# RMSNorm and SiLU: 1/rms by ScalarE's Sqrt and VectorE's reciprocal instead of GpSimd's pow

## The chip, the cores and the metric

One core of a Trainium2 chip. The metric is device time in microseconds for one execution of the program. PE is TensorE, DVE is VectorE, ACT is ScalarE, POOL is GpSimd, and SP is SyncE, which here issues loads. ACTq and SPq are the instruction queues of ACT and SP where they issue DMAs.

## The reference

```python
def reference(x, gamma, eps):          # x: 8 x 1024 x 2048 float32, gamma: 2048, eps: 1e-5
    rms = np.sqrt(np.mean(x ** 2, axis=-1, keepdims=True) + eps)
    out = gamma * x / rms
    return (out * (1 / (1 + np.exp(-out)))).astype(np.float32)
```

Each of 8192 rows of 2048 numbers is divided by its root mean square and scaled by gamma, and SiLU is applied to the result.

## The kernel before

The 8192 rows are cut into 16 blocks of 512 rows. A block is one tile `xt` of 128 partitions, each with J = 4 rows of 2048 numbers side by side: 4096 KB. There are six such buffers, and everything happens in place in them. A block is loaded by one DMA that SP issues (`load`, L52) and stored by one DMA that ACT issues (`store`, L91); only the last block is stored in two halves (L88).

`sums(b)` makes the sum of squares of each row. Its rows are shared out: the first `na` rows go to ACT (Square with an accumulated sum, into the PSUM tile `junk_a`, L68), the others to DVE (a multiply with an accumulated sum, into `junk_v`, L64). `na` is 2, but 3 in blocks 1, 5, 9 and 13. The four sums are in `ss`, 128x4. POOL then computes `var = ss / 2048 + eps` (L74) and `rstd = var ** -0.5` (L77, with a constant tile `half` that holds -0.5).

`finish(b)` multiplies each row by its rstd and by gamma on DVE (`scalar_tensor_tensor`, L82, four per block); after every second row ACT applies Silu to the two rows together (L86, 128x4096, two per block).

The order is written out by hand, and each engine works through its own instructions in that order:

```python
for b in range(1, last - 1):
    sums(b + 1, after_first=[b - 1])
    finish(b)
```

So the sums of block b+1, and its rstd, come ahead of the scaling of block b: rstd is there one block ahead. The store of block b-1 is issued by ACT just after its first square of block b+1, and when a store has landed, SP can issue the load of the block six further on, into the same buffer. At the start six loads are issued (the sixth after gamma has been spread over all partitions by TensorE, with `grow` in the sixth buffer). At the end the order is: store 13, finish 14, store 14, sums 15, finish 15 with its two halves.

Of the kernel before, what the change touches and what calls it, by code (L numbers as in the profile page):

```python
# [1 line left out]

# [4 lines left out]

ACT = mybir.ActivationFunctionType
ALU = mybir.AluOpType


@with_exitstack
def kernel(
    ctx: ExitStack,
    tc: tile.TileContext,
    x: bass.AP,
    gamma: bass.AP,
    eps: bass.AP,
    out: bass.AP,
):  # L20

    nc = tc.nc
    P = nc.NUM_PARTITIONS
    f32 = mybir.dt.float32
    x2 = x.flatten_outer_dims()
    o2 = out.flatten_outer_dims()  # L30
    n, d = x2.shape
    J = 4
    BUFS, LEAD = 6, 6
    nblk = n // (P * J)
    xb = x2.rearrange("(b p j) d -> b p (j d)", p=P, j=J)
    ob = o2.rearrange("(b p j) d -> b p (j d)", p=P, j=J)

    singles = ctx.enter_context(tc.tile_pool(name="singles", bufs=1))
    pool = ctx.enter_context(tc.tile_pool(name="pool", bufs=BUFS))
    small = ctx.enter_context(tc.tile_pool(name="small", bufs=2))  # L40
    psum = ctx.enter_context(tc.tile_pool(name="psum", bufs=1, space=bass.MemoryType.PSUM))

    g = singles.tile([P, d], f32)
    half = singles.tile([P, J], f32)
    ones = singles.tile([P, P], f32)
    junk_a = psum.tile([P, d], f32, name="junk_a")
    junk_v = psum.tile([P, d], f32, name="junk_v")
    blocks, rstds = {}, {}

    def load(b):  # L50
        xt = pool.tile([P, J * d], f32, name="xt")
        nc.sync.dma_start(out=xt, in_=xb[b])  # L52
        blocks[b] = xt

    def row(b, j):
        return blocks[b][:, j * d:(j + 1) * d]

    def sums(b, after_first=()):


        ss = small.tile([P, J], f32, name="ss")
        na = J - 1 if b % 4 == 1 else J - 2
        for j in range(na, J):
            nc.vector.tensor_tensor_reduce(  # L64
                out=junk_v, in0=row(b, j), in1=row(b, j), scale=1.0, scalar=0.0,
                op0=ALU.mult, op1=ALU.add, accum_out=ss[:, j:j + 1])
        for j in range(na):
            nc.scalar.activation(out=junk_a, in_=row(b, j), func=ACT.Square,  # L68
                                 accum_out=ss[:, j:j + 1])
            if j == 0:  # L70
                for s in after_first:
                    store(s)
        var = small.tile([P, J], f32, name="var")
        nc.gpsimd.tensor_scalar(out=var, in0=ss, scalar1=1.0 / d, scalar2=float(eps),  # L74
                                op0=ALU.mult, op1=ALU.add)
        rstd = small.tile([P, J], f32, name="rstd")
        nc.gpsimd.tensor_tensor(out=rstd, in0=var, in1=half, op=ALU.pow)  # L77
        rstds[b] = rstd

    def finish(b, halves=False):  # L80
        for j in range(J):
            nc.vector.scalar_tensor_tensor(out=row(b, j), in0=row(b, j), scalar=rstds[b][:, j:j + 1],  # L82
                                           in1=g, op0=ALU.mult, op1=ALU.mult)
            if j % 2:
                cols = slice((j - 1) * d, (j + 1) * d)
                nc.scalar.activation(out=blocks[b][:, cols], in_=blocks[b][:, cols], func=ACT.Silu)  # L86
                if halves:
                    nc.scalar.dma_start(out=ob[b][:, cols], in_=blocks[b][:, cols])  # L88

    def store(b):  # L90
        nc.scalar.dma_start(out=ob[b], in_=blocks[b])  # L91
        if b + LEAD < nblk:
            load(b + LEAD)

    with tc.manual_schedule():


        Q = 4
        w = d // Q
        grow = pool.tile([P, J * d], f32, name="xt")  # L100
        for b in range(BUFS - 1):
            load(b)
        nc.vector.memset(ones, 1.0)  # L103
        nc.gpsimd.memset(half, -0.5)  # L104
        nc.scalar.activation(out=junk_a[:, 0:1], in_=ones[:, 0:1], func=ACT.Square)  # L105
        nc.scalar.dma_start(out=grow[0:P:P // Q, 0:w],
                            in_=bass.AP(tensor=gamma.tensor, offset=gamma.offset, ap=[[w, Q], [1, w]]))
        for c in range(Q):
            k = c * (P // Q)
            nc.tensor.matmul(junk_v[:, c * w:(c + 1) * w], ones[k:k + 1, :], grow[k:k + 1, 0:w],  # L110
                             start=True, stop=True)
        nc.vector.tensor_copy(out=g, in_=junk_v)  # L112
        load(BUFS - 1)


        last = nblk - 1
        sums(0)
        finish(0)
        sums(1)
        for b in range(1, last - 1):  # L120
            sums(b + 1, after_first=[b - 1])
            finish(b)
        store(last - 2)
        finish(last - 1)
        store(last - 1)
        sums(last)
        finish(last, halves=True)


# [1 line left out]
_INS = ['x', 'gamma', 'eps']  # L131
_OUTS = [((8, 1024, 2048), 'float32')]

_NUMBERS = {'eps': 9.999999747378752e-06}


# [26 lines left out]
```

## Time and profile before

| what | value |
|---|---|
| median of 9 runs | 317.86 us (317.4 to 318.82) |
| profiled execution | 318.03 us, of which 315.9 us is the span of the profile |
| DVE busy | 212.6 us, 67% |
| ACT busy | 190.3 us, 60% |
| POOL busy | 64.6 us, 20% |
| moved by DMA | 134.24 MB, mean 425 GB/s |
| table loads on ACT | 2, 1.283 us each |

The span runs from the first instruction to the last. Busy shares are means over it. A row of the groups gives the line, the engine, the operation, its tiles and shapes, how often it ran, and the mean duration of one.

### The profile page before, as it was taken

How to read it: one execution, taken by the hardware profiler on the slowest of the kernel's cores; microseconds unless marked ns; L12 is line 12 of the kernel's file. 1: busy time of each engine (PE TensorE's matmuls, PEld its weight loads, DVE VectorE, ACT ScalarE, POOL GpSimd, SP SyncE). 2: the span in 40 equal slices, each digit the busy share in tenths (PEclk: the TensorE clock that was granted, in tenths of full speed). 3: DMA queues.
4: the chain of work that ended last, by engine and by line, in shares of the span. 5: the costliest groups of instructions: out<-in, count | busy, mean ns of one | idle time of the engine just before them, and what ended most of it. 6: DMA issues, size and time to landing. Idle time of an engine off the chain costs nothing.

```text
span 315.9 us, 446 instructions
## 1 busy us (share of the span) xinstructions
PE 2.1 (1%) x8; PEld 0.5 (0%) x8; DVE 212.6 (67%) x122; ACT 190.3 (60%) x107; POOL 64.6 (20%) x37
## 2 busy tenths in 40 slices
PE   0200000000000000000000000000000000000000
PEld 0000000000000000000000000000000000000000
DVE  0688699996672956929577294893939549993700
ACT  1338978688774295463877438557378843784620
POOL 0010160514040500605104060140601306001000
DMA  8999999999999999999999999999999999999996
GB/s 333 411 452 423 440 398 415 448 436 427 448 415 452 408 445 419 448 415 448 415 461 407 456 415 448 415 452 427 436 427 436 427 436 431 432 440 423 444 409 280
DMA packets 4762, 134.24 MB, mean 425 GB/s; under 512 B 532, under 2 KB 532, under 8 KB 536
## 3 DMA queue, kind: packets, MB, share of 16 engines
q1 hardware_dynamic: 2304, 67.11, 49.6%
q10 hardware_dynamic: 2456, 67.12, 49.3%
q14 instruction: 2, 0.02, 0.0%
HBM read 67.12 MB, written 67.11 MB: 425 GB/s over the span
## 4 chain that ended last, share of the span: by engine, by line
DMA 69%; DVE 9%; ACT 3%; issue 2%; DVEq 1%; POOLq 0%; ACTq 0%; POOL 0%; SPq 0%
DMA xt<-in_x_dram 37%; DMA out_dram<-xt 32%; DVE xt L82 8%; ACT xt L86 2%; ACT junk_a L68 1%; DVE junk_v L64 1%; DVEq L158 1%; POOLq L158 0%; ACTq L91 0%; DVE ss L64 0%; POOL var L74 0%; ACTq L68 0%; SPq L52 0%; DVEq L82 0%; DVEq L64 0%
## 5 line engine op out<-in xcount | busy, mean ns | idle before, releaser
L86 ACT ACTIVATE xt<-xt 128x4096 f32<-128x4096 f32 x32 | 115.8, 3618 | 71.4 <-DVE xt L82 71.4
L82 DVE SCALAR_TENSOR_TENSOR xt<-xt,rstd,g 128x2048 f32<-128x2048 f32 x64 | 146.1, 2347 | 8.7 <-POOL rstd L77 8.7
L64 DVE CUSTOM_DVE_ANT_0 junk_v<-xt 128x2048 f32<-128x2048 f32 x28 | 64.4, 2300 | 67.1 <-DMA xt<-in_x_dram 66.6
L68 ACT ACTIVATE junk_a<-xt 128x2048 f32<-128x2048 f32 x36 | 67.7, 1880 | 39.6 <-DMA xt<-in_x_dram 38.5
L74 POOL TENSOR_SCALAR var<-ss 128x4 f32<-128x4 f32 x16 | 22.4, 1401 | 222.7 <-DVE ss L64 118.1
L77 POOL TENSOR_TENSOR rstd<-var,half 128x4 f32<-128x4 f32 x16 | 41.9, 2621 | 1.3
L112 DVE COPY g<-junk_v 128x2048 f32<-128x2048 f32 x1 | 2.3, 2293 | 9.3 <-PE junk_v L110 9.3
L68 ACT ACTIVATION_READ_ACCUMULATOR junk_a<-xt 128x1 f32 x36 | 6.7, 187 | 0.0
L64 DVE DVE_READ_ACCUMULATOR2_ANT ss<- 128x1 f32 x28 | 4.0, 142 | 0.0
L110 PE MATMUL junk_v<-xt,ones 1*128 1x512 f32 x8 | 2.1, 1132 | 8.1 <-DMA xt<-in_gamma_dram 8.1
L105 ACT ACT_TABLE_LOAD x1 | 1.3, 1283 | 0.7 <-PEq L144 0.7
L86 ACT ACT_TABLE_LOAD x1 | 1.3, 1283 | 0.0
L103 DVE MEMSET ones<- 128x128 f32 x1 | 0.2, 165 | 0.8 <-PEq L144 0.8
L110 PEld LDWEIGHTS junk_v<-xt,ones 1*128 1x128 f32 x8 | 0.5, 305 | 8.1 <-issue 8.1
L105 ACT ACTIVATE junk_a<-ones 128x1 f32<-128x1 f32 x1 | 0.2, 174 | 0.0
L104 POOL MEMSET half<- 128x4 f32 x1 | 0.1, 102 | 0.3 <-POOLq L144 0.3
L144 POOL MEMSET const-float32-0.0<- 128x1 f32 x1 | 0.1, 99 | 0.2 <-issue 0.2
L144 POOL MEMSET const-bfloat16-1.0<- 128x1 bf16 x1 | 0.1, 102 | 0.0
L144 POOL MEMSET const-uint8-127<- 128x1 uint8 x1 | 0.1, 102 | 0.0
L144 POOL MEMSET const-float32-1.0<- 128x1 f32 x1 | 0.1, 99 | 0.0
## 6 DMA issues: line engine op xcount, KB each, us to landing
xt<-in_x_dram SPq DMA_DIRECT2D x16, 4096.0 KB, 38.4
out_dram<-xt ACTq DMA_DIRECT2D x15, 4096.0 KB, 38.6
out_dram<-xt ACTq DMA_DIRECT2D x2, 2048.0 KB, 12.6
xt<-in_gamma_dram ACTq DMA_DIRECT2D x1, 8.0 KB
```

The source lines that it names most:

```text
L64: nc.vector.tensor_tensor_reduce(out=junk_v, in0=row(b, j), in1=row(b, j), scale=1.0, scalar=0.0, op0=ALU.mult, op1=ALU.add, accum_out=ss[ ...
L68: nc.scalar.activation(out=junk_a, in_=row(b, j), func=ACT.Square, accum_out=ss[:, j:j + 1])
L74: nc.gpsimd.tensor_scalar(out=var, in0=ss, scalar1=1.0 / d, scalar2=float(eps), op0=ALU.mult, op1=ALU.add)
L77: nc.gpsimd.tensor_tensor(out=rstd, in0=var, in1=half, op=ALU.pow)
L82: nc.vector.scalar_tensor_tensor(out=row(b, j), in0=row(b, j), scalar=rstds[b][:, j:j + 1], in1=g, op0=ALU.mult, op1=ALU.mult)
L86: nc.scalar.activation(out=blocks[b][:, cols], in_=blocks[b][:, cols], func=ACT.Silu)
L103: nc.vector.memset(ones, 1.0)
L105: nc.scalar.activation(out=junk_a[:, 0:1], in_=ones[:, 0:1], func=ACT.Square)
L110: nc.tensor.matmul(junk_v[:, c * w:(c + 1) * w], ones[k:k + 1, :], grow[k:k + 1, 0:w], start=True, stop=True)
L112: nc.vector.tensor_copy(out=g, in_=junk_v)
L144: nc = _bacc.Bacc("TRN2", target_bir_lowering=False, num_devices=1)
L158: with _tile.TileContext(nc) as tc:
```

## The change

POOL's two operations are replaced. ACT computes `rms = sqrt(ss / 2048 + eps)` at the end of `sums` (eps is a one-column tile, set once by DVE), and a new function `invert` has DVE take the reciprocal. In the loop `invert(b + 1)` stands after `finish(b)`; for blocks 0, 1 and 15 it stands just after `sums`. All blocks now have two rows of squares on ACT and two on DVE. POOL keeps only the constants that the program's start sets.

```diff
-    half = singles.tile([P, J], f32)
+    eps_t = singles.tile([P, 1], f32)
...
-        na = J - 1 if b % 4 == 1 else J - 2
+        na = J // 2
...
-        var = small.tile([P, J], f32, name="var")
-        nc.gpsimd.tensor_scalar(out=var, in0=ss, scalar1=1.0 / d, scalar2=float(eps),
-                                op0=ALU.mult, op1=ALU.add)
+        rms = small.tile([P, J], f32, name="rms")
+        nc.scalar.activation(out=rms, in_=ss, func=ACT.Sqrt, scale=1.0 / d, bias=eps_t)
+        rmss[b] = rms
+
+    def invert(b):
         rstd = small.tile([P, J], f32, name="rstd")
-        nc.gpsimd.tensor_tensor(out=rstd, in0=var, in1=half, op=ALU.pow)
+        nc.vector.reciprocal(out=rstd, in_=rmss.pop(b))
         rstds[b] = rstd
...
-        nc.gpsimd.memset(half, -0.5)
+        nc.vector.memset(eps_t, float(eps))
...
         sums(0)
+        invert(0)
         finish(0)
         sums(1)
+        invert(1)
         for b in range(1, last - 1):
             sums(b + 1, after_first=[b - 1])
             finish(b)
+            invert(b + 1)
         store(last - 2)
         finish(last - 1)
         store(last - 1)
         sums(last)
+        invert(last)
         finish(last, halves=True)
```

More of the change, by code (lines that the diff above doesn't have):

```diff
@@ L47 @@
     junk_v = psum.tile([P, d], f32, name="junk_v")
-    blocks, rstds = {}, {}
+    blocks, rmss, rstds = {}, {}, {}
     def load(b):
```

## The prediction

> **What bounds the kernel now.** I read the page's busy shares first, then its slices, then stretches of the span by windows, then the order of time inside one block and at the end.
>
> Busy time of each engine, from the page, and the busy share of the 16 DMA engines in 40 slices:
>
> ```profile
> PE 2.1 (1%) x8; PEld 0.5 (0%) x8; DVE 212.6 (67%) x122; ACT 190.3 (60%) x107; POOL 64.6 (20%) x37
> DMA  8999999999999999999999999999999999999996
> ```
>
> No compute engine is full; the DMA engines are, from the second slice to the last but one. 134.24 MB must pass. The windows (busy us by engine, clock, DMA share, GB/s) say how full:
>
> ```profile
> 10.00:38.00 28.00, 0.23 (x4) 0.00 (x0) 23.14 (x15) 18.41 (x13) 1.21 (x2) 1.00 1.01 437
> 38.00:62.00 24.00, 0.00 (x0) 0.00 (x0) 22.54 (x12) 18.78 (x12) 10.58 (x6) 1.00 0.99 415
> 100.80:256.80 156.00, 0.00 (x0) 0.00 (x0) 104.98 (x60) 93.94 (x52) 38.03 (x16) 1.00 1.00 433
> ```
>
> 437 GB/s while only loads run, 415 when the first stores join, 433 for the long middle. A block is one load and one store of 4096 KB, 8.39 MB, and 8.39 MB at 433 GB/s is 19.4 us. The middle runs at just that pace, as the order of time of one block shows (start, length, what; the idle time before it in brackets):
>
> ```profile
> 198.86 1.88 ACT L68 ACTIVATE junk_a<-xt 128x2048 f32<-128x2048 f32 x1 [1.91 <-DMA xt<-in_x_dram]
> 198.89 2.30 DVE L64 CUSTOM_DVE_ANT_0 junk_v<-xt 128x2048 f32<-128x2048 f32 x1 [5.58 <-DMA xt<-in_x_dram]
> 203.50 9.14 DVE L82 SCALAR_TENSOR_TENSOR xt<-xt,rstd,g 128x2048 f32<-128x2048 f32 x4
> 205.98 2.99 POOL L77 TENSOR_TENSOR rstd<-var,half 128x4 f32<-128x4 f32 x1
> 208.15 3.62 ACT L86 ACTIVATE xt<-xt 128x4096 f32<-128x4096 f32 x1 [5.25 <-DVE xt L82]
> 212.67 3.62 ACT L86 ACTIVATE xt<-xt 128x4096 f32<-128x4096 f32 x1 [0.91 <-DVE xt L82]
> 218.20 1.88 ACT L68 ACTIVATE junk_a<-xt 128x2048 f32<-128x2048 f32 x1 [1.91 <-DMA xt<-in_x_dram]
> ```
>
> A load lands at 198.86, the next at 218.20: 19.34 us. In between DVE squares until 203.5 and scales until 212.65, ACT's second Silu ends at 216.29, and then both wait for the next load. The waits put 66.6 us (DVE) and 38.5 us (ACT) down to loads. The pow on POOL belongs to the next block, whose scaling starts one load later, at 222.84: it has 13.9 us to spare.
>
> The end, by the same view:
>
> ```profile
> 287.68 0.19 ACT L68 ACTIVATION_READ_ACCUMULATOR junk_a<-xt 128x1 f32 x1
> 287.95 0.20 POOL L74 TENSOR_SCALAR var<-ss 128x4 f32<-128x4 f32 x1 [20.96 <-ACT junk_a L68]
> 288.23 1.01 POOL L77 TENSOR_TENSOR rstd<-var,half 128x4 f32<-128x4 f32 x1
> 289.27 9.14 DVE L82 SCALAR_TENSOR_TENSOR xt<-xt,rstd,g 128x2048 f32<-128x2048 f32 x4 [4.91 <-POOL rstd L77]
> 297.57 0.34 ACTq L88 DMA_DIRECT2D out_dram<-xt  x1
> 302.10 0.34 ACTq L88 DMA_DIRECT2D out_dram<-xt  x1
> ```
>
> Here rstd is waited for: squares end at 287.87, scaling starts at 289.27, 1.40 us later. But the DMA is still busy. From 297.6 until the rate drops to nothing at about 313.1 the windows add up to 6.55 MB; the two half blocks are 4.19 MB; so 2.36 MB, 5.4 us at 433 GB/s, were queued ahead of the first half. It landed 12.5 us after its issue: 5.4 of queue, 4.8 of its own 2.10 MB, and 2.3 of latency. If all of that latency were lost behind an empty queue, the cover would be 5.4 − 2.3 = 3.1 us. So the last halves may come 3.1 to 5.4 us later before the end moves.
>
> **The change, part by part.**
>
> *POOL's two operations go.* 22.4 + 41.9 = 64.3 us of busy time, all beside other work in the middle. At the start (block 0) and at the end they are on the way to the scaling, 1.4 to 1.5 us each time. At the start the scaling of block 0 is hidden behind six loads in flight, at the end behind the queued stores. Worth nothing by itself.
>
> The trace has POOL's pow at 2.99 us beside DVE work and at 1.01 us while DVE waits, and DVE's 64 scalings at 2344 to 2352 ns, beside POOL or not. So DVE pays nothing for POOL and gains at most 8 ns in 2347.
>
> The Trainium skill (GPSIMD Engine Reference, section Specifications) says that GpSimd shares its SBUF interfaces with VectorE and contends with DVE instructions of two SBUF inputs, which would make POOL's absence a gain for the scaling. This trace shows that contention on POOL's side alone; by the rule at its strongest DVE would get faster, and DVE has 5.6 us to spare in each block anyway.
>
> *ACT gets Sqrt and its table switches.* The built order has 31 table loads where there were 2: one ahead of each Sqrt but one, one ahead of the Silus of each block but block 14 (whose Silus follow block 13's directly). 29 × 1.283 us (the table load's row) = 37.2 us. Sixteen Sqrt of 128x4: no row shows one. The nearest is the 128x1 activation, 0.17 us; the far one the 128x2048, 1.88 us; I take 0.19. That is 3.0 us. Minus four squares moved to DVE, 4 × 2.07 = 8.3 us. ACT goes from 190.3 to about 222 us, 70% of the span.
>
> In a middle block: the Sqrt's table load waits, in the built program, for DVE's last sum, 4.65 us after the load lands. It ends at 5.95, Sqrt at 6.2, Silu's table load at 7.5. The first Silu waits for two scalings in any case, until 9.29 (208.15 − 198.86). The 5.25 us of idle time ahead of it hide all this; with the Sqrt at its far end (1.88) the table is there at 9.2, still in time. What stands behind the Sqrt on ACT is only these Silus; the store of the block before has been issued already, with the first square. Uncovered, a delay at the first Silu reaches the second only after 0.91 us more, and the store only after another 1.9 us.
>
> The Trainium skill (ScalarE: Activation LUTs, section What ACT_TABLE_LOAD costs) speaks against this edit: 1283 ns plus a drain of 1380 ns for every switch, so functions of one set belong together. The trace has the 1283 ns; a drain it does not show, since the load at 17.00 starts 0.01 us after the instruction before it. By the page's figure two switches take 5.3 us per block, the first Silu starts about 1 us late, the second not at all, and the forecast is the same.
>
> *DVE gets the reciprocal.* No row shows it; the smallest DVE operations take 0.14 and 0.17 us, the far row is 2.35 us; I take 0.14, near a 128x4 operand. In a middle block it stands after the four scalings, 13.8 us after the load landed, and Sqrt is long done; behind it are the next block's squares, which wait for a load until 19.34. Hidden, at the far end too (16.1).
>
> *Squares two and two.* Blocks 1, 5, 9, 13 had one square on DVE and three on ACT. 4 × 2.44 = 9.8 us more on DVE (to about 225 us, 71%). Those blocks' Silus now end 17.4 instead of about 15.0 us after the load, like all others, still 1.9 us ahead of the next load. Nothing.
>
> *The ramp, blocks 1 to 4.* Here compute sets the order, since the loads are ahead. Following the built order with these durations: invert(1) now holds DVE until Sqrt of block 1 at 37.3 before it squares block 2; the scaling of block 1 starts at 42.2 instead of 39.4. Store 0 is issued at 37.3 (38.15 before), stores 1, 2, 3 at 55.0, 69.3, 83.5 (52.25, 65.9, 81.5): up to 3.4 us later. From block 5 on the loads pace again. While these stores are late, loads 0 to 5 (the last landed at 81.4) and load 6, issued when store 0 lands (62.1), keep the DMA full: bytes change places, none are lost. Without that backlog it would cost up to 3.4 us. What the trace can't tell is whether another interleaving has another rate: 38 to 62 moved 415 GB/s, 433 less 415 over 24 us is 1.0 us. If the ramp loses nothing it is −1.0; if twice as much, +1.0. I take 0, since the pattern stays one of loads joined by stores.
>
> *The end.* Squares end, then table load 1.28, Sqrt 0.19, reciprocal 0.14, hand-overs 0.08 + 0.05 (rows: 0.08 ACT to POOL, 0.04 POOL to DVE): 1.74 instead of 1.40, +0.34. invert(14) ahead of block 14's scaling adds 0.14. Together +0.5 us against a cover of 3.1 to 5.4. Silu's table load hides under two scalings (4.6 us). Far ends: 1.28 + 1.88 + 2.35 + 0.13 − 1.40 + 2.35 = +6.6.
>
> *Sum.* The profiled execution took 318.03 us, 315.9 of span and 2.1 around it; 0.17 above the median of the nine runs. Start 0, middle 0, ramp 0 (−1.0 to +1.0), end 0 (up to +3.5): 318.0 for that execution, **317.9** on the median.
>
> **The rivals.**
>
> *The end is uncovered (slower).* If the last rstd comes more than 3.1 to 5.4 us later than now, the DMA runs dry and the excess adds. At both far ends, 6.6 − 3.1 = 3.5 us, 321.4; with only one of the two small operations at its far end the delay is 2.2 (Sqrt) or 4.9 us (both reciprocals), the latter 1.8 us over the lower bound, 319.7. Against: a 128x4 operand is far nearer to the 0.14 to 0.19 us rows. 6%.
>
> *The ramp loses more (slower)*, 318.9, or *less (faster)*, 316.9, from the changed order of stores. For: the 415 GB/s stretch is real, and the stores move by up to 3.4 us. Against: totals elsewhere are 431 to 437 for every mix. 10% each.
>
> *POOL leaves the last chain (faster).* The chain that ended last runs through POOL; taking 1.4 us off would give 316.5. It needs the end to be uncovered now and Sqrt plus reciprocal to be free. 4%.
>
> *The change doesn't do what it says:* rstd was one block ahead before as well; only the place of the reciprocal is new. That leaves the forecast as it is.
>
> **How the numbers follow.** No change 70%, end uncovered 6%, ramp 10% and 10%, POOL's 4%. A measurement of this kernel tells about 0.2% (0.6 us) from no change; within no change the median may still fall a little outside. Some of the ramp's cases stay within 0.6. Faster 0.15, same 0.68, slower 0.17. The range takes in the ramp's ends and stops short of the end's far ends: 316.9 to 319.1.
>
> **What would show it.** Right: DMA slices of 9 throughout, loads landing every 19.3 us in the middle, 31 table loads of 1.28 us with the first Silu still starting 9.3 us after the load, ACT near 222 and DVE near 225 us, the last halves issued near 298.1 and 302.6, data until 313. Wrong: Silus that wait for table loads, a gap in the DMA after 300, or a ramp whose 38 to 62 stretch moves much more or less than 415 GB/s.

## The result, and the profile after

| | median | runs | standard deviation | profiled execution, span |
|---|---|---|---|---|
| before | 318.18 us | 63 (317.39 to 319.53) | 0.59 us | 318.03, 315.9 |
| after | 317.64 us | 19 (317.27 to 317.91) | 0.18 us | 317.34, 315.5 |

The ratio is 0.9979, with a 95% interval of 0.9969 to 0.9988: about 0.2% faster, 0.54 us between the medians and 0.68 us between the means. The forecast was no change at 317.9 us. That 317.64 lies so near to it is partly luck: the forecast rests on a nine-run median of 317.86 us, and 63 runs of the same kernel give 318.18. Two of the twelve executions of late_shift4 below (323.02 and 323.32 us), over 1.5% above its fastest, are left out of its median, deviation and ratio.

Every run's time is its span plus a part outside the span, before the first or after the last instruction. In the 19 runs of after that part is 1.80 us (1.74 to 1.84). In the profiled execution of before it is 2.12, and in 122 runs of before that were taken beside the experiments 2.10 (2.05 to 2.16). So of the 0.54 us some 0.3 us lie outside the span, and only the rest, 0.2 us between medians or 0.4 between means, lies inside it. The best runs hardly differ (317.39 and 317.27); what went inside the span is the upper part of the spread. There are two questions, then: what took 0.3 us off the part outside, and where the spread of the spans comes from.

The page of the kernel after:

```profile
PE 2.1 (1%) x8; PEld 0.5 (0%) x8; DVE 223.5 (71%) x147; ACT 223.8 (71%) x144; POOL 0.2 (0%) x4
DMA  8999999999999999999999999999999999999997
```

and its costs of the new operations (line, operation, shapes, count, busy us, mean ns, idle before):

```profile
L74 ACT ACT_TABLE_LOAD x15 | 19.2, 1283 | 9.9 <-DVE ss L64 9.8
L88 ACT ACT_TABLE_LOAD x15 | 19.2, 1283 | 3.1 <-DVE xt L84 2.9
L79 DVE RECIPROCAL rstd<-rms 128x4 f32<-128x4 f32 x16 | 2.8, 173 | 11.3 <-ACT rms L74 11.3
L74 ACT ACTIVATE rms<-ss,eps_t 128x4 f32<-128x4 f32 x16 | 4.8, 298 | 1.2 <-DVE ss L64 1.1
```

ACT has 33.5 us more work, DVE 10.9 us more, POOL 64.4 us less, and the DMA row reads as before but for its last slice. One middle block in order of time, with the load that SP issues when a store has landed:

```profile
196.68 19.73 SPq L52 DMA_DIRECT2D xt<-in_x_dram  x2
200.67 1.88 ACT L68 ACTIVATE junk_a<-xt 128x2048 f32<-128x2048 f32 x1 [1.85 <-DMA xt<-in_x_dram]
205.61 1.28 ACT L74 ACT_TABLE_LOAD   x1 [0.90 <-DVE ss L64]
206.91 0.30 ACT L74 ACTIVATE rms<-ss,eps_t 128x4 f32<-128x4 f32 x1
207.22 1.28 ACT L88 ACT_TABLE_LOAD   x1
210.04 3.62 ACT L88 ACTIVATE xt<-xt 128x4096 f32<-128x4096 f32 x1 [1.53 <-DVE xt L84]
214.56 3.62 ACT L88 ACTIVATE xt<-xt 128x4096 f32<-128x4096 f32 x1 [0.91 <-DVE xt L84]
```

Both table loads fit, and the first Silu still waits 1.53 us for DVE. What is new stands in the first two lines. A store has landed at 196.68 (SP issues the load that waited for it), a load at 200.67: the store is 3.99 us ahead. In the kernel before, the same two events are

```profile
199.00 19.69 SPq L52 DMA_DIRECT2D xt<-in_x_dram  x2
```

and the load landing at 198.86 that the prediction shows: 0.14 us behind. I call this number (SP's issue of a load, less ACT's first square next to it, near 200 us) the *distance*: +0.14 before, −3.99 after. In these two kernels it stays about the same through the middle (+0.11 to +0.16 and −3.7 to −4.0 from 100 to 240 us), since each store is issued when a load lands and each load when a store lands. A block takes 19.3 us, so a distance of −4 can also be read as 15.3 us behind the load before.

The first store of all, store 0, is issued at another time. Before, then after:

```profile
38.15 0.36 ACTq L91 DMA_DIRECT2D out_dram<-xt  x1
36.63 0.35 ACTq L93 DMA_DIRECT2D out_dram<-xt  x1
```

### The profile page after: what moved, and what is told of

Its sections match the earlier page's. It is cut to its first block, busy times and chain, and to the rows that moved or that the text cites. A ratio compares the mean times of both kernels' runs of the same rounds, so it can differ in the third digit from the quotient of the medians.

```text
span 315.5 us, 444 instructions
## 1 busy us (share of the span) xinstructions
PE 2.1 (1%) x8; PEld 0.5 (0%) x8; DVE 223.5 (71%) x147; ACT 223.8 (71%) x144; POOL 0.2 (0%) x4
## 4 chain that ended last, share of the span: by engine, by line
DMA 66%; DVE 18%; ACT 8%; issue 3%; DVEq 1%; ACTq 0%; SPq 0%
DMA xt<-in_x_dram 44%; DMA out_dram<-xt 22%; DVE xt L84 14%; ACT xt L88 5%; DVE junk_v L64 4%; ACT junk_a L68 2%; ACT L74 1%; DVEq L164 1%; ACT rms L74 0%; DVE rstd L79 0%; DVE ss L64 0%; ACTq L93 0%; SPq L52 0%; DVEq L64 0%; ACTq L74 0%
## 5 line engine op out<-in xcount | busy, mean ns | idle before, releaser
L64 DVE CUSTOM_DVE_ANT_0 junk_v<-xt 128x2048 f32<-128x2048 f32 x32 | 73.5, 2298 | 55.8 <-DMA xt<-in_x_dram 55.2
L68 ACT ACTIVATE junk_a<-xt 128x2048 f32<-128x2048 f32 x32 | 60.1, 1879 | 29.0 <-DMA xt<-in_x_dram 28.0
L79 DVE RECIPROCAL rstd<-rms 128x4 f32<-128x4 f32 x16 | 2.8, 173 | 11.3 <-ACT rms L74 11.3
L68 ACT ACTIVATION_READ_ACCUMULATOR junk_a<-xt 128x1 f32 x32 | 6.0, 187 | 0.0
L74 ACT ACTIVATE rms<-ss,eps_t 128x4 f32<-128x4 f32 x16 | 4.8, 298 | 1.2 <-DVE ss L64 1.1
```

Of the source, the lines that this page charges most:

```text
L64: nc.vector.tensor_tensor_reduce(out=junk_v, in0=row(b, j), in1=row(b, j), scale=1.0, scalar=0.0, op0=ALU.mult, op1=ALU.add, accum_out=ss[ ...
L74: nc.scalar.activation(out=rms, in_=ss, func=ACT.Sqrt, scale=1.0 / d, bias=eps_t)
L79: nc.vector.reciprocal(out=rstd, in_=rmss.pop(b))
```

## The experiments

All times are beside runs of the kernel before on the same chip. The theories: *POOL* (its work costs the 0.2%), *later blocks* (the split in blocks 5, 9, 13), *first store* (store 0's issue time sets the distance, and the distance the time), and, of the cause behind the last, *addresses*, *queues* and *tie*, each told where it is tested. Several expectations lie only 0.2% apart, about as wide as the intervals, so I look at the standard deviation and the spans too.

**again**: the kernel before, against itself.

> The kernel before, unchanged, timed against itself: how far two identical programs come apart, and where a slower execution has its extra time. No theory expects a difference: ratio 1.000, within 0.001. The times of the kernel before spread from 317.4 to 319.5 us, those of the kernel after only from 317.3 to 317.9; the same spread should show here, and the profile of this run, if it is a slower one, should show whether the extra time lies in the ramp (10 to 100 us), in the middle or at the end (after 300 us).

318.34 us, ratio 0.9997 (0.9977 to 1.0017), standard deviation 0.51. The profiled execution took 318.59, span 316.5, with a distance of +1.72. So the distance differs between two executions of one program, and the spread belongs to that program. The extra time is not in the middle (433 GB/s again).

**split_only**: before, with

```diff
-        na = J - 1 if b % 4 == 1 else J - 2
+        na = J // 2
```

> The kernel before with squares split two and two on all blocks; POOL's pow stays. Theory POOL (POOL's work beside the transfers costs the 0.2%): ratio 1.000, 318.2 us. Theory order of the ramp (later stores in blocks 1 to 4 move the landings of loads and stores apart, which coincide before: 198.86 and 198.98): DVE squares block 1 twice, so the scaling of block 1 starts about 2 us later; if that moves the landings of loads and stores apart by some us, ratio 0.998, if they still coincide, 1.000.

317.74 us, 0.9975 (0.9957 to 0.9994), with POOL at work. Store 0 went out at 36.61, distance −4.09. That is as large a gain as the change's, without Sqrt, and all of it is inside the span: the median span is 315.65 us, against 316.10 in the runs of before beside it.

**sqrt_only**: after, with the old split (that diff the other way round).

> The kernel after with the old split (three squares on ACT in blocks 1, 5, 9, 13). Theory POOL: POOL is idle, so all of the gain, ratio 0.998. Theory order of the ramp: block 1 is scaled at another time than in both kernels, so the ratio follows the distance between the landings of stores and loads in the middle: near 0.1 us as before gives 1.000, near 4 us as after gives 0.998.

318.25 us, 0.9998 (0.9974 to 1.0023), standard deviation 0.92, store 0 at 38.61, distance +2.03. Idle POOL, Sqrt and reciprocal alone bring nothing in sum: the part outside the span is 1.77 us here, 0.3 less than before, but the median span is 316.5 us against 316.1, a difference within the spread of these runs. The profiled execution was a long one, 320.45 us, with only 428 GB/s in the middle.

**pool_idle_work**: after, plus POOL's two operations for nobody.

```diff
+    half = singles.tile([P, J], f32)
...
+        var = small.tile([P, J], f32, name="var")
+        nc.gpsimd.tensor_scalar(out=var, in0=ss, scalar1=1.0 / d, scalar2=float(eps),
+                                op0=ALU.mult, op1=ALU.add)
+        idle = small.tile([P, J], f32, name="idle")
+        nc.gpsimd.tensor_tensor(out=idle, in0=var, in1=half, op=ALU.pow)
...
+        nc.gpsimd.memset(half, -0.5)
```

> The kernel after, with POOL doing its two old operations on every block's sums again, for nobody (tiles var and idle, which nothing reads). Theory POOL: the gain goes, ratio 1.000 and the wide spread of the kernel before comes back. Theory order of the ramp: stays at 0.998 with a narrow spread, since no store moves.

318.07 us, 0.9989 (0.9970 to 1.0007), distance −2.99, standard deviation 0.37. Between the two expectations, and the spans tell why. Inside the span nothing is lost clear of the runs' spread (median 315.95 us, 315.9 after). The part outside is back at 2.10 us (2.06 to 2.15), where after has 1.80 (1.74 to 1.84). The same holds for all kernels here: the eleven rows of the table below in which POOL does its two operations on every block have 2.05 to 2.16 us outside the span in each single run, the six in which it does not have 1.74 to 1.84. So POOL's work costs 0.3 us, outside the span. Which part of the program's start or end that is, the traces do not show. Inside the span POOL is not needed for a gain: split_only, and store0_36 below, have it with POOL at work.

**split_block1** and **split_rest**: before, with the split changed in block 1 alone, and in 5, 9, 13 alone.

```diff
-        na = J - 1 if b % 4 == 1 else J - 2
+        na = J - 1 if b in (5, 9, 13) else J - 2     # split_block1
+        na = J - 1 if b == 1 else J - 2              # split_rest
```

> The kernel before with two squares on each engine in block 1 only; blocks 5, 9 and 13 keep three on ACT. Theory first store (the split acts through block 1 alone: ACT reaches store 0 at 36.6 instead of 38.15, and from then on each store lands some 4 us ahead of a load instead of with it): all of the gain of the kernel with the full split, 317.7 us, ratio 0.9975 to 0.998, landings 4 us apart, spread below 0.4. Theory later blocks (squares of blocks 5, 9, 13): ratio 1.000, spread 0.5 to 0.9.

> The kernel before with two squares on each engine in blocks 5, 9 and 13; block 1 keeps three on ACT. Theory first store: store 0 stays at 38.15, landings within 2 us of each other, ratio 1.000, spread 0.5 or more. Theory later blocks: 0.9975 to 0.998.

Block 1 alone: 317.58 us, 0.9988 (0.9976 to 1.0000), distance −3.37, standard deviation 0.32. The others alone: 317.92 us, 0.9992 (0.9977 to 1.0007), distance +2.31, standard deviation 0.55. The ratios do not separate the two; distance and standard deviation do, and they go with block 1. But split_block1's profiled execution, at a distance of −3.37, took 318.39 us, the longest of its twelve runs: a distance on that side does not make every execution a short one.

**store0_early** and **store0_late**: only store 0 is moved, in the kernel before to an earlier place, in the kernel after to a later one.

```diff
# store0_early
-        sums(1)
+        sums(1, after_first=[0])
         for b in range(1, last - 1):
-            sums(b + 1, after_first=[b - 1])
+            sums(b + 1, after_first=[b - 1] if b > 1 else [])
# store0_late
-            if j == 0:
+            if j == (1 if b == 2 else 0):
                 for s in after_first:
                     store(s)
```

> The kernel before with store 0 alone issued earlier, after the first square of block 1 (about 32 us) instead of the first of block 2 (38.15); no arithmetic is moved. Theory first store: landings move at least 4 us apart (6 to 10), so at least the gain of the split, ratio 0.998 or below. Theory POOL and theory later blocks: 1.000, since neither POOL nor a square is touched.

> The kernel after with store 0 alone issued later, after the second square of block 2 (about 40 us) instead of at 36.63; POOL stays idle, the squares stay two and two. Theory first store: landings come back to within 2 us of each other, the gain goes, ratio 1.000 and the spread widens to 0.5 or more. Theory POOL, and theory later blocks: 0.998 stays.

Early (32.25 us): 317.66 us, 0.9988 (0.9976 to 1.0000), standard deviation 0.22, distance −11.91, which is also 7.4 us behind the load before. Late (40.05 us): 322.19 us, 1.0132 (1.0112 to 1.0151), far worse than expected: one DMA issued 3.4 us later cost 4.5 us. The distance became +3.85 near 180 us (+3.62 near 200):

```profile
180.08 1.88 ACT L68 ACTIVATE junk_a<-xt 128x2048 f32<-128x2048 f32 x1 [2.40 <-DMA xt<-in_x_dram]
183.93 20.14 SPq L52 DMA_DIRECT2D xt<-in_x_dram  x2
```

and the windows (DMA share and GB/s in the last two columns) show both where the time went, a slower middle and a long tail:

```profile
100.80:256.80 156.00, 0.00 (x0) 0.00 (x0) 110.29 (x72) 111.52 (x72) 0.00 (x0) 1.00 1.00 426
314.00:316.00 2.00, 0.00 (x0) 0.00 (x0) 0.00 (x0) 0.00 (x0) 0.00 (x0) 1.00 0.96 410
316.00:318.00 2.00, 0.00 (x0) 0.00 (x0) 0.00 (x0) 0.00 (x0) 0.00 (x0) 1.00 0.54 229
318.00:320.00 2.00, 0.00 (x0) 0.00 (x0) 0.00 (x0) 0.00 (x0) 0.00 (x0) 1.00 0.08 33
```

The share stays 1.00 while the rate falls from 433 to 426: the DMA engines are not idle, their packets take longer. At the end the share falls off in steps: some of the 16 engines are done and others are not.

**late_shift4** and **after_shift4**: store0_late and after, with loads from 16 rows further on.

```diff
-        nc.sync.dma_start(out=xt, in_=xb[b])
+        r = b * P * J + (16 if b < nblk - 1 else 0)
+        nc.sync.dma_start(out=xt, in_=x2[r:r + P * J].rearrange("(p j) d -> p (j d)", p=P))
```

> The run with store 0 late (322.2 us), but every block except the last is loaded from 16 rows (four partitions, 128 KB) further on in x, so the rows computed are others; times of issue and sizes are as they were. Theory addresses (the transfers slow down because the load stream and the store stream, 3.85 us apart in landing, are at unlucky addresses relative to each other): four partitions are half of the eight that one of 16 DMA engines has in a block, some 9.7 us of distance, so the slow case becomes a fast one, 317.7 us, ratio 0.998 to 1.000. Theory queues (what counts is how many loads and stores wait in the two queues when one of them lands): stays at 322 us, ratio 1.013.

> The kernel after with the same shift of its loads (other rows are computed). Theory addresses: the fast distance of -4 us becomes another one by 9.7 us, so its time should move, to 318 to 322 us, unless that distance happens to be a fast one too. Theory queues: 317.6 us as without the shift, ratio 0.998.

The late one stayed slower than before, 1.006 (1.0031 to 1.0088), between the two expectations, and its runs fell into two groups, 318.1 to 319.2 and 321.4 us and up. The shifted kernel after stayed at 317.66 us, 0.9986 (0.9973 to 0.9999), standard deviation 0.17: the address theory had expected it to move, unless the new distance happens to be a good one too. The shift also moved the distances, to +2.75 and −2.05, so it did not change addresses alone. The fast case gives no sign of an effect of addresses; in the slow one they may have a part.

**before_late**: before, with store 0 late (the second diff of store0_late).

> The kernel before with store 0 alone issued later, after the second square of block 2 (about 40 us instead of 38.15); POOL's pow and the three squares stay. Theory distance of the landings (whatever its cause, addresses or queues): stores land 3 us or more behind loads, and the time goes to 319 to 322 us, ratio 1.003 to 1.013, without Sqrt or any table load. Theory that the late store hurts only together with ACT's table loads: ratio 1.000.

322.07 us, 1.013 (1.0109 to 1.0151); five of six runs at 321.7 us or more, and the profiled one 318.58, at a distance of +2.99. So the loss needs no Sqrt and no table load, and near +3 one program can run either way.

**after_early**: after, with store 0 early (the first diff of store0_early).

> The kernel after with store 0 issued after the first square of block 1 (about 32.6 us instead of 36.63). Theory distance of the landings: still further on the good side, about -10 to -12 us; 317.5 us, ratio 0.998, spread 0.2, so the change of arithmetic adds nothing to what the early store alone gives the kernel before (317.66 us). A theory in which idle POOL or the split has a gain of its own would give 317.1 us or less, ratio below 0.997.

317.38 us, 0.9976 (0.9963 to 0.9989), standard deviation 0.29, distance −5.72, not the −10 to −12 expected. It is the lowest median of all, 0.28 us below store0_early's. The median spans of the two are alike, 315.60 and 315.55 us; the difference is the part outside, 1.77 against 2.10. So idle POOL does have a gain of its own, smaller than the bound of 317.1 that was set for it.

**store0_36**: before, with store 0 1.7 us earlier and nothing else changed.

```diff
-            if j == 0:
+            if j == (2 if b == 1 else 0):
...
-        sums(1)
+        sums(1, after_first=[0])
         for b in range(1, last - 1):
-            sums(b + 1, after_first=[b - 1])
+            sums(b + 1, after_first=[b - 1] if b > 1 else [])
```

> The kernel before with store 0 alone issued about 2 us earlier, after the third square of block 1 (about 36.1 us instead of 38.15); squares, POOL, and the order of everything else stay. Theory distance of the landings: stores land 3 to 4 us ahead of loads, 317.6 us, ratio 0.998, spread below 0.35: the whole gain of the change from the move of one DMA. If the gain needs the split, Sqrt or an idle POOL: ratio 1.000, spread 0.5 to 0.7.

317.54 us, 0.9980 (0.9965 to 0.9995), standard deviation 0.10, the steadiest of all. In its order of time store 0 is here

```profile
36.41 0.36 ACTq L91 DMA_DIRECT2D out_dram<-xt  x1
195.92 0.33 SPq L52 DMA_DIRECT2D xt<-in_x_dram  x1
200.84 1.88 ACT L68 ACTIVATE junk_a<-xt 128x2048 f32<-128x2048 f32 x1 [1.93 <-DMA xt<-in_x_dram]
```

instead of at 38.15, and near 200 us a store has landed at 195.92 and a load at 200.84, a distance of −4.92. POOL is busy for 65.0 us, three squares of block 1 are on ACT, and there is no Sqrt. The move of this one DMA gives as much as the whole change (0.9979), and all of it inside the span: the median span is 315.45 us, against 316.30 in the runs of before beside it, and the part outside is 2.09.

**before_free** and **late_free**: before and before_late, with stores 1 to 13 issued by their own block's end, no longer behind a load's landing.

```diff
-            sums(b + 1, after_first=[b - 1])
+            sums(b + 1, after_first=[0] if b == 1 else [])
             finish(b)
-        store(last - 2)
+            store(b)
```

> The kernel before with stores 1 to 13 issued right after their own block's Silu, some 2 us before the next load lands, instead of just after it; store 0 stays at 38.15. Theory tie (a store that waits for a load's last engine spreads the engines): ratio 0.997 to 0.998, spread below 0.35, with landings still within 2 us of each other. Theory distance alone: the distance is as in the kernel before, so ratio 1.000, spread 0.5 or more.

> The run with the kernel before and store 0 late (322.1 us), with stores 1 to 13 issued right after their own block's Silu. Theory tie: the loss goes, 317.7 to 318.2 us, ratio 0.998 to 1.000. Theory distance alone: the distance stays at +3 us or more, 321 to 322 us, ratio 1.010 to 1.013.

318.68 us, 1.0013 (0.9997 to 1.0029), distance +1.54; and 320.74 us, 1.0081 (1.0044 to 1.0117), distance +2.64. Cutting the tie leaves before as it was. The late case lies between its two expectations, five of its twelve runs at 318.7 to 319.2 us and the others from 320.2 to 323.4, so the loss does not go with the tie. The distances stay on the side that store 0's place gives them, with or without it.

All runs, in order of the issue of store 0, on several chips, so that small differences between medians mean nothing. "Outside" is the mean of time less span (for before, of the 122 runs beside the experiments):

| kernel | store 0, us | distance, us | median, us | standard deviation | outside, us | profiled: span | spread at the end |
|---|---|---|---|---|---|---|---|
| store0_early | 32.25 | −11.91 | 317.66 | 0.22 | 2.10 | 315.4 | 0.3 |
| after_early | 32.54 | −5.72 | 317.38 | 0.29 | 1.77 | 315.6 | 1.3 |
| split_block1 | 36.20 | −3.37 | 317.58 | 0.32 | 2.11 | 316.3 | 1.9 |
| store0_36 | 36.41 | −4.92 | 317.54 | 0.10 | 2.09 | 315.4 | 1.0 |
| split_only | 36.61 | −4.09 | 317.74 | 0.38 | 2.11 | 315.8 | 1.4 |
| after | 36.63 | −3.99 | 317.64 | 0.18 | 1.80 | 315.5 | 1.3 |
| pool_idle_work | 36.83 | −2.99 | 318.07 | 0.37 | 2.10 | 315.8 | 1.3 |
| after_shift4 | 37.02 | −2.05 | 317.66 | 0.17 | 1.79 | 316.1 | 1.5 |
| before | 38.15 | +0.14 | 318.18 | 0.59 | 2.10 | 315.9 | 1.6 |
| again | 38.25 | +1.72 | 318.34 | 0.51 | 2.10 | 316.5 | 2.1 |
| split_rest | 38.30 | +2.31 | 317.92 | 0.55 | 2.11 | 317.0 | 2.7 |
| before_free | 38.40 | +1.54 | 318.68 | 0.57 | 2.11 | 317.1 | 2.8 |
| sqrt_only | 38.61 | +2.03 | 318.25 | 0.92 | 1.77 | 318.7 | 3.0 |
| store0_late | 40.05 | +3.62 | 322.19 | 0.39 | 1.77 | 320.6 | 3.5 |
| late_free | 40.26 | +2.64 | 320.74 | 1.87 | 2.11 | 320.6 | 4.2 |
| late_shift4 | 40.40 | +2.75 | 319.14 | 1.51 | 1.79 | 317.2 | 2.8 |
| before_late | 40.41 | +2.99 | 322.07 | 1.52 | 2.11 | 316.5 | 1.9 |

The last column is read from the trace's completion marks: each load and each store ends with 16 marks, which I take as one of each of the 16 DMA engines, and this is the time from the first to the last of the 16 for the last store. Span and spread at the end go together: from 1.0 to 2.8 us of spread the span grows from 315.4 to 317.2 us, one for one; beyond, it grows faster, and there the middle is slower too (428, 426, 427 GB/s). The span ends 0.9 to 1.0 us after the last mark. So a longer execution is one in which the 16 engines end apart; the kernel waits for the last of them.

The spread in the middle does not tell as much. In store0_36 it is 0.95 to 1.1 us at every landing from 118 us on. But in after it is 1.7 to 1.9 in the middle and 1.25 at the end, where before has 1.6 to 1.7 and 1.6; and in after_shift4, whose median is 317.66 us, stores land 3.1 us apart all through the middle, and only 1.5 at the end. What the runs with stores 1.5 to 4 us behind the loads have in common is growth: the spread of the stores goes from 2.5 us at store 0 to 4.1 in store0_late, from 2.3 to 3.6 in split_rest, from 2.1 to 2.8 in again; in before_late it is that of the loads, from 1.2 to 3.1. It is not theirs alone, since the stores of split_block1 have it too (2.2 to 2.95).

What is shown: the issue time of store 0, moved by itself, gives a gain inside the span (store0_36, store0_early) and a large loss (store0_late, before_late); POOL's two operations, put back by themselves, cost 0.3 us outside it (pool_idle_work). The change does both, it moves store 0 and empties POOL, and its gain is made of both. Whether Sqrt and its table loads take a part of the first back (the median span is 315.9 us after, 315.65 in split_only) these runs can't tell. What is only seen together, in one profiled execution of each kernel: distance, spread of the engines, time. What stays open: why engines end apart when stores land with the loads or a few us after them. The tie between the queues is not the cause by itself, and nothing points to address alone; the DMA engines' order of packets was not tried.

## Why the prediction was wrong, point by point

*The bound* was right: the DMA is full from 10 to 313 us, and the middle moves 433 GB/s in both kernels. After:

```profile
100.80:256.80 156.00, 0.00 (x0) 0.00 (x0) 110.40 (x72) 113.17 (x73) 0.00 (x0) 1.00 1.00 433
```

*Middle blocks* were right. The first Silu starts 9.37 us after the load landed (9.3 was given), ACT has 223.8 us (222), DVE 223.5 (225). Sqrt takes 0.298 us where I took 0.19 and the reciprocal 0.173 where I took 0.14; both lie near the rows I chose them by. The Trainium skill (ScalarE: Activation LUTs, What ACT_TABLE_LOAD costs) gives 280 ns plus 0.833 ns per element for an activation with a bias from a tile, 283 ns here, nearer to the 298 measured than my row. Its drain of 1380 ns per switch does not show: the table load that starts at 205.61 ends at 206.89 and Sqrt starts at 206.91, and the next table load starts 0.01 us after Sqrt.

*POOL* is one of the two steps that failed. "Worth nothing by itself" holds inside the span: store0_36 has POOL's 65 us and a gain as large. But the sum added "2.1 around it" to the span and gave no reason why these 2.1 us should stay. They fell to 1.80 us (1.77 to 1.80 in all six kernels with idle POOL) and are back at 2.10 with POOL's operations put back. That is 0.3 us of the 0.54, in a term that the prediction carried over unchanged.

*The end* was right in kind. From the last square to the scaling it takes 1.85 us (1.74 was given, 1.40 before):

```profile
289.78 0.19 ACT L68 ACTIVATION_READ_ACCUMULATOR junk_a<-xt 128x1 f32 x1
291.28 0.30 ACT L74 ACTIVATE rms<-ss,eps_t 128x4 f32<-128x4 f32 x1
291.82 9.14 DVE L84 SCALAR_TENSOR_TENSOR xt<-xt,rstd,g 128x2048 f32<-128x2048 f32 x4
300.12 0.34 ACTq L90 DMA_DIRECT2D out_dram<-xt  x1
304.64 0.34 ACTq L90 DMA_DIRECT2D out_dram<-xt  x1
```

The last halves came 2.5 us later than before, not 0.5, because the loads land some 2 us later now; they landed 9.8 us after issue in place of 12.6, so the cover took it, and data still ended at 313.

*The ramp* is the other step that failed. Its times were right: stores 0 to 3 were given for 37.3, 55.0, 69.3, 83.5 and came at 36.63, 55.78, 69.75, 83.88. "Bytes change places, none are lost" held for the ramp itself (38 to 62: 416 GB/s, 415 before). But I priced the new order only by that stretch, "I take 0, since the pattern stays one of loads joined by stores", and looked no further. The 1.5 us by which store 0 came earlier put every later landing of a store ahead of its load, and that distance lasts through the middle. In place of 0, moves of store 0 by themselves gave −0.85 us (store0_36) and −0.35 us (store0_early) in the median span against before, and the change itself, all its parts together, some −0.2 to −0.4. For the same reason *squares two and two* was not nothing: in block 1 it takes one square of 2 us from ACT's way to store 0. The rival that named the order of stores had the place and, in its faster half, the sign, not the mechanism or the size; its 1.0 us was the rate of the ramp.

I also read the nine times of before (317.4 to 318.82) as noise of the measurement. They were for the most part a property of the kernel: after, the standard deviation falls from 0.59 to 0.18 us.

## What to carry to other kernels

In a kernel that keeps two DMA queues full, the issue time of the first store can set how the two streams lie to each other for the rest of the run; before an edit in the ramp is costed at nothing, follow which landings it moves and by how much. A wide spread of a kernel's own times is a sign of such a state, and moving one DMA by a few microseconds is a cheap experiment. Where a change of arithmetic brings a small gain in a kernel that the DMA bounds, try its side effect on DMA order alone before the gain is put down to the arithmetic. And split each run's time into its span and the part outside it: here that alone shows that an operation off the critical path still cost 0.3 us.

## What the runs showed of the hardware

The rate of a full DMA is not one number: 433 GB/s with stores landing about 4 us ahead of loads (after), 426 with stores 3.85 us behind (store0_late), at a busy share of 1.00 in both. The 16 completion marks of the last store lie 0.3 to 4.2 us apart, and the spread can build up over a run (2.5 to 4.1 us in store0_late). Executions of one program can differ widely (before_late: 318.58 to 323.29 us). Programs in which GpSimd works on every block have 2.05 to 2.16 us of time outside their span, those in which it does not 1.74 to 1.84.
